# Shift and scale columns from raw fp32 blocks as stationary operand, and a tile-by-tile pipeline for the first k and v products

## The chip, the cores and the metric

The kernel runs on one NeuronCore of a Trainium2 chip. The core has a matrix engine (TensorE, PE in the profile; PEld is its loading of the stationary operand), VectorE (DVE), ScalarE (ACT), GpSimd (POOL) and SyncE (SP), which here only issues transfers; 16 DMA engines move the data. The metric is the device time of one launch in microseconds, lower is better. The runs of a kernel are summed up by their median.

## The reference, cut to what matters

One layer of a hybrid model over 1280 rows (1024 latent tokens and 256 context tokens) of 1024 features. The part that the change touches is the beginning:

```
cond_ = silu(cond)                       # two vectors: c (latent), c_ctx (context)
mod   = cond_ @ w_ada + b_ada            # 1024 x 6144; sh1, sc1, gt1, sh2, sc2, gt2
u     = rmsnorm(x, g_norm1) * (1 + sc1) + sh1
proj  = u @ w_in                         # xp, su, sv, q, k, v, o_pre, gate_pre, br_pre
```

Behind it follow a pooling branch, a spatial gating branch and a four-head mLSTM (whose gates are in gate_pre, and whose first step needs k, v and q of head 0), the merge, and a feed-forward block. All of it is fp32; the products are made from split operands, a rounded high part and a low part.

## The kernel before

**Tiling.** The rows stand in ten row tiles of 128 (`xt[0]` to `xt[9]`), in three groups: 512 rows (tiles 0 to 3), 512 (4 to 7) and 256 (8 and 9, the context). The features stand in eight feature tiles of 128 (k = 0 to 7). A feature tile of a group is made in four steps: row tiles are scaled by their norm (`scale_rows`: ACT squares and sums, DVE adds, POOL takes the power, DVE scales); PE transposes 128x128 pieces into a PSUM tile `pt_u` (`transpose_cols`); ACT writes `val_u` = `pt_u` * a + sh, with one scale and one shift for each feature; DVE splits it into `u..h` and `u..l` (`modulate_cols`). ACT also issues the transfer of `val_u` to `scr_u` in DRAM, for later stages.

**Products.** `dense` makes, for a weight matrix split into hi and lo (`load_w`), three products a feature tile: hi*h, hi*l, lo*h. In the trace they are `p_k` and `p_v`, 512 columns for groups 0 and 1 and 256 for group 2.

**Shift and scale.** Only the first 2048 columns of w_ada are needed for the first modulation: blocks 0 and 1 are the shift of feature tiles 0 to 3 and 4 to 7, blocks 2 and 3 the scale of the same tiles. SP fetches them in the order 0, 2, (weights of k0), 1, 3, each as eight tiles `wa` of 128x512 (256 KB). Each block is handled in two steps. `mod_split(b)`: ACT rounds a `wa` tile into `wah`, DVE (POOL for two tiles in eight) subtracts to `wal`, and PE multiplies with the two conditioning columns (`shl`, `sh0`) as the stationary operand: two products of 512 columns a tile into `pm`. `mod_cols(b)`: ACT copies the row result to `mrow`, four small fp32 products (`pmc`) turn it into columns, and DVE adds the bias (`sh1`) or makes (1+sc)*g (`a1`).

**Order.** From line 248 to 297 the engines are wrapped in `Pinned` (line 44 in the trace is its call): each engine takes its instructions in the order of the code. Behind line 297 a scheduler sets the order. The pinned part handles group 0 alone. Behind it come the split of the gate weights, the transfers, scaling and modulation of row tiles 4 to 9 (lines 304 to 310), the gate product `pg` (lines 322 to 331), and a chain of small steps on DVE and ACT that ends in the transposes `pc` (line 396). k0 and v0 of groups 1 and 2 are made in `head_proj(0)`, beside that chain.

Of the kernel before, what the change touches and what calls it, by code (L numbers as in the profile page):

```python
# [49 lines left out]
def hybrid_step(  # L50
# [38 lines left out]

    def load_w(src, name, raw=None, eng=V):  # L90
        raw = fetch_w(src, name) if raw is None else raw
        hi = wp.tile([P, 1024], F32R, tag="hi", name=f"hi_{name}", bufs=NHL)
        lo = wp.tile([P, 1024], F32R, tag="lo", name=f"lo_{name}", bufs=NHL)
        A.copy(hi, raw)
        eng.tensor_tensor(lo, raw, hi.bitcast(F32), ALU.subtract)
        return hi, lo
# [21 lines left out]
    def dense(ps, w, acts, g, ks=range(KT)):  # L118
        n = GROUPS[g][1]
        whi, wlo = w  # L120
        for k in ks:
            ahi, alo = acts[k][g]
            s = slice(k * P, (k + 1) * P)
            PE.matmul(ps[:, :n], whi[:, s], ahi, start=k == 0, stop=False)
            PE.matmul(ps[:, :n], whi[:, s], alo, start=False, stop=False)
            PE.matmul(ps[:, :n], wlo[:, s], ahi, start=False, stop=k == KT - 1)
# [35 lines left out]
    def norm_rows(x, n, name):  # L162
        sq = small([P, 2], f"sq_{name}")
        for hf in (0, 1):
            junk = tmp(f"junk_{name}{hf}")
            A.activation(junk, x[:, hf * 512 : hf * 512 + 512], AF.Square, accum_out=sq[:, hf : hf + 1])
# [4 lines left out]
    def transpose_cols(src, g, k, name):
        ps = ps_sd(f"pt_{name}{g}_{k}")
        for i in range(GROUPS[g][1] // P):
            PE.transpose(ps[:, i * P : (i + 1) * P], src[i][:, k * P : (k + 1) * P], ident)
        return ps

    def modulate_cols(dst, ps, g, k, a, sh, name):
        n, j = GROUPS[g][1], 1 if g == 2 else 0
        val = tmp(f"val_{name}{g}_{k}")
        A.activation(val[:, :n], ps[:, :n], AF.Identity, bias=sh[:, k, j : j + 1], scale=a[:, k, j : j + 1])  # L180
        if g < 2:
            A.dma_start(scr_u[g][k], val)
# [4 lines left out]
    def scale_rows(g):
        for i in range(GROUPS[g][0] // P, (GROUPS[g][0] + GROUPS[g][1]) // P):
            r = norm_rows(xt[i], 1, f"x{i}")
            V.tensor_scalar(xt[i], xt[i], r[:, 0:1], None, ALU.mult)  # L190

    ada = {}
    for b in (0, 2, 1, 3):
        if b == 1:
            raw_k0 = fetch_w(w_in[I_K], "k0")
        for k in range(KT):
            ada[b, k] = slot(f"wa{b}_{k}", F32)
            SP.dma_start(ada[b, k], w_ada[k * P : (k + 1) * P, b * 512 : (b + 1) * 512])
# [21 lines left out]
    def mod_split(b, ks=range(KT), behind=2):  # L220
        if b not in pms:
            pms[b] = ps_sd(f"pm{b}")
        pm = pms[b]
        for k in ks:
            wh, wl = slot(f"wah{b}_{k}"), slot(f"wal{b}_{k}")
            A.copy(wh, ada[b, k])
            (G if k in POOL_LO else V).tensor_tensor(wl, ada[b, k], wh.bitcast(F32), ALU.subtract)
            PE.matmul(pm[0:4, :], shl[:, k, :], wh, start=k == 0, stop=False)
            los.append((k, wl))
            while los and (k == KT - 1 or los[0][0] <= k - behind):  # L230
                k2, w2 = los.pop(0)
                PE.matmul(pm[0:4, :], sh0[:, k2, :], w2, start=False, stop=k2 == KT - 1)

    def mod_cols(b):
        half = b % 2
        kk = slice(half * 4, half * 4 + 4)
        mrow = mrows[half][0:4, (b // 2) * 512 : (b // 2 + 1) * 512]
        A.copy(mrow, pms[b][0:4, :])
        pmc = ps_mm(f"pmc{b}")
# [3 lines left out]
        dst = sh1 if b < 2 else a1
        V.tensor_tensor(dst[:, kk, :], pmv, bav[:, b * 4 : b * 4 + 4, :], ALU.add)
        if b >= 2:
            V.scalar_tensor_tensor(a1[:, kk, :], a1[:, kk, :], 1.0, g1v[:, kk, :], ALU.add, ALU.mult)

    V, A, G, PE = (Pinned(tc, e) for e in engines)
    scale_rows(0)
    u0 = [None] * KT  # L250

    def tr(k):
        u0[k] = transpose_cols(xt[0:4], 0, k, "u")

    def mc(k):
        modulate_cols(uT, u0[k], 0, k, a1, sh1, "u")

    mod_split(0)
    mod_split(2, (0, 1))
    mod_cols(0)  # L260
# [36 lines left out]
    V, A, G, PE = engines
    wgh = wp.tile([P, KT, 100], F32R, tag="hi", name="wg_hi", bufs=NHL)
    wgl = wp.tile([P, KT, 100], F32R, tag="lo", name="wg_lo", bufs=NHL)
    for i in range(2):  # L300
# [1 line left out]
        tc.keep_in_program_order(A.copy(wgh[:, ks], wg[i]))
        tc.keep_in_program_order(V.tensor_tensor(wgl[:, ks], wg[i], wgh[:, ks].bitcast(F32), ALU.subtract))
    for i in range(4, NT):
        SP.dma_start(xt[i], xs[i])
    for g in (1, 2):
        scale_rows(g)
        t0, n = GROUPS[g]
        for k in range(KT):
            modulate_cols(uT, transpose_cols(xt[t0 // P : (t0 + n) // P], g, k, "u"), g, k, a1, sh1, "u")  # L310
# [144 lines left out]
    hn2 = [z[:, 9010 + i * 512 : 9522 + i * 512].rearrange("p (c t) -> p c t", t=P) for i in range(2)]  # L455

    def proj(idx, name, evict, eng=V):
        w, ps = begun.pop(name, (None, None))
        w = w or load_w(w_in[idx], name, eng=eng)
        for g in range(3):  # L460
            if ps is None or g > 0:
                ps = ps_mm(f"p_{name}{g}")
                dense(ps, w, uT, g)
            evict(g, ps)

    def head_proj(h):
        tiles = {}
        kq = slot(f"kq{h}", F32)
        for nm, idx, sc in (("k", I_K, float(P) ** -0.5), ("v", I_V, 1.0), ("q", I_Q, 1.0)):
            lst = tiles[nm] = []  # L470

            def ev(g, ps):
                n = GROUPS[g][1]
                if g == 2 and nm != "v":
                    t = kq[:, 0:256] if nm == "k" else kq[:, 256:512]
                else:
                    t = slot(f"{nm}T{h}_{g}", F32)
                A.activation(t[:, :n], ps[:, :n], AF.Copy, scale=sc)
                lst.append(t)

            proj(idx + h, f"{nm}{h}", ev)
# [965 lines left out]
```

## Time and profile before

| what | value |
| --- | --- |
| median of three runs | 1984.17 us (1979.58 to 1986.23) |
| the profiled execution | 1989.21 us |
| its span | 1987.40 us |
| its mean granted PE clock | 0.989 |
| the chain that ended last | PE 40%, DVE 3%, DMA 2%, ACT 1% of the span |

The chain that ended last is work followed back from the last instruction; its share is mostly PE. The page's table of 40 slices gives the busy share in tenths: the first slice of 50 us and the last are those in which PE is not full.

```profile
PE   5999999999899999999999999999999999999997
PEclk9999999999999999999999998999999999999999
```

A line of the timeline reads: start and duration in microseconds, engine, line of the code, operation, output tile<-input tiles, shapes, count, and in brackets the idle time before it and what ended that.

### The profile page before, as it was taken

What the parts mean: (1) busy time and instruction counts of PE and PEld (TensorE: products, weight loads), DVE (VectorE), ACT (ScalarE), POOL (GpSimd) and SP (SyncE); (2) the same over time, 40 slices, a digit from 0 to 9 for tenths busy, and PEclk for the clock granted to TensorE, in tenths of its full rate; (3) what the DMA queues carried; (4) which work ended last, traced back from release to release, by engine and by line L of the source; (5) the groups of instructions that cost most, each with busy time, mean ns of one, the idle gap of its engine ahead of it and who ended that gap; (6) DMA issues with size and microseconds to landing.
All of it is one profiled execution on the core that took longest, in us unless ns stands there. A gap on an engine that the chain in (4) does not pass through costs nothing. (4 is left out here: it accounts for less than half of the span.)

```text
span 1987.4 us, 29215 instructions
## 1 busy us (share of the span) xinstructions
PE 1923.3 (97%) x10544; PEld 1656.8 (83%) x10544; DVE 1332.6 (67%) x2269; ACT 858.1 (43%) x1780; POOL 382.5 (19%) x372
## 2 busy tenths in 40 slices
PE   5999999999899999999999999999999999999997
PEld 2788888998778888878889998888888878888886
DVE  6684344448878979774566689888776654654664
ACT  6543454653143333331014565554445544443443
POOL 3000001116402324330000005445441110000002
PEclk9999999999999999999999998999999999999999
DMA  8211111112564545469634535776774586655544
GB/s 341 86 45 38 48 59 42 40 57 85 175 228 145 169 142 176 133 210 345 234 122 149 170 139 186 271 260 237 249 275 142 190 324 210 197 177 155 165 134 148
DMA packets 160642, 332.70 MB, mean 167 GB/s; under 512 B 18929, under 2 KB 41329, under 8 KB 158449
## 3 DMA queue, kind: packets, MB, share of 16 engines
q1 hardware_dynamic: 107280, 224.30, 34.6%
q10 hardware_dynamic: 38976, 52.97, 7.4%
q0 software_dynamic: 14240, 53.56, 7.3%
q8 instruction: 83, 1.36, 0.3%
q14 instruction: 63, 0.51, 0.1%
HBM read 229.53 MB, written 101.22 MB: 166 GB/s over the span
## 5 line engine op out<-in xcount | busy, mean ns | idle before, releaser
L1155 POOL TENSOR_TENSOR z<-z 128x512 f32<-128x512 f32 x64 | 98.7, 1543 | 133.7 <-DMA z<-in_w_ff 131.0
L885 DVE TENSOR_TENSOR z<-z 128x512 f32<-128x512 f32 x112 | 92.2, 824 | 2.5
L445 POOL PARTITION_ALL_REDUCE acc<-acc x16 | 55.0, 3474 | 188.5 <-DVE acc L439 117.6
L439 DVE SCALAR_TENSOR_TENSOR acc<-z,scond,acc 128x512 f32<-128x512 f32 x112 | 85.9, 815 | 0.0
L1269 POOL TENSOR_TENSOR rs_y<-rs_y,neghalf 128x1 f32<-128x1 f32 x10 | 9.4, 940 | 333.6 <-DVE rs_y L1268 333.6
L1121 ACT ACTIVATE z<-z 128x512 f32<-128x512 f32 x64 | 40.5, 632 | 76.4 <-DVE z L894 36.7
L910 ACT ACTIVATE z<-z 128x512 f32<-128x512 f32 x48 | 30.2, 632 | 71.8 <-DVE z L894 27.7
L819 ACT CAST hi_wb<-raw_wb 128x512 fp32r<-128x512 f32 x24 | 14.8, 620 | 100.7 <-PE pb L987 67.2
L131 POOL TENSOR_TENSOR rs_h<-rs_h,neghalf 128x4 f32<-128x4 f32 (+1 forms) x12 | 11.9, 992 | 207.9 <-DVE rs_h L130 207.8
L992 DVE TENSOR_TENSOR sg<-pb,sg 128x512 f32<-128x512 f32 (+1 forms) x48 | 28.9, 602 | 33.0 <-PE pb L988 31.6
L582 DVE SCALAR_TENSOR_TENSOR yc<-th,ccol,z 128x512 f32<-128x512 f32 (+1 forms) x12 | 7.9, 660 | 57.2 <-PE th L580 57.2
L1122 ACT ACTIVATE z<-z 128x512 f32<-128x512 f32 x64 | 40.3, 630 | 1.1
L670 POOL TENSOR_TENSOR z<-z 128x1024 f32<-128x1024 f32 (+13 forms) x20 | 34.8, 1750 | 14.0 <-ACT z L654 12.5
L819 ACT CAST hi_wo<-raw_wo 128x512 fp32r<-128x512 f32 x48 | 28.8, 616 | 19.9 <-PE po L1087 13.6
L1090 DVE TENSOR_TENSOR po<-po,gt 128x256 f32<-128x256 f32 x40 | 17.2, 430 | 29.3 <-PE po L1088 29.2
L1146 POOL DMA_DIRECT2D scr_s<-x x48 | 26.3, 551 | 52.0 <-DVE x L1140 47.3
L446 POOL TENSOR_TENSOR acc<-acc,bt 1x512 f32<-1x512 f32 x16 | 23.8, 1500 | 59.0 <-issue 59.0
L820 DVE TENSOR_TENSOR lo_wo<-raw_wo,hi_wo 128x512 fp32r<-128x512 f32 x48 | 32.2, 686 | 3.6 <-ACT hi_wo L819 3.6
L44 PE MATMUL pm<-wah,shl 128*4 128x512 f32 x32 | 14.7, 479 | 17.2 <-DVE s_x L44 12.5
L1093 ACT ACTIVATE po<-z 128x256 f32<-128x256 f32 x40 | 15.4, 385 | 36.9 <-DVE z L1092 35.7
L516 DVE SCALAR_TENSOR_TENSOR z<-z,dmb,kv 128x129 f32<-128x129 f32 x56 | 16.3, 344 | 21.9 <-PE kv L505 21.6
L569 DVE TENSOR_TENSOR den<-den,gcol 128x2 f32<-128x2 f32 x40 | 6.2, 159 | 35.2 <-ACT den L568 34.4
(5091 smaller groups left out, 7466.7 us busy)
## 6 DMA issues: line engine op xcount, KB each, us to landing
z<-in_w_ff SPq DMA_DIRECT2D x64, 512.0 KB, 5.5
z<-in_w_ada SPq DMA_DIRECT2D x64, 256.0 KB, 3.3
scr_t<-z POOLq DMA_DIRECT2D x16, 1024.0 KB, 4.6
z<-in_w_in SPq DMA_DIRECT2D x24, 512.0 KB, 4.4
scr_g<-z ACTq DMA_DIRECT2D x48, 256.0 KB, 2.0
sg<-scr_g SPq DMA_DIRECT2D x48, 256.0 KB, 4.6
raw_wo<-in_w_out SPq DMA_DIRECT2D x48, 256.0 KB, 3.5
scr_h<-z ACTq DMA_DIRECT2D x48, 256.0 KB, 4.0
```

The costliest lines, as they stand in the source:

```text
L439: V.scalar_tensor_tensor(acc[j], raw, scond[:, k, j : j + 1], acc[j], ALU.mult, ALU.add)
L445: G.partition_all_reduce(acc[j], acc[j], P, bass.bass_isa.ReduceOp.add)
L670: eng.tensor_tensor(at(dst, a, b), at(src, a - l, b - l), at(src, a + r_, b + r_), ALU.add)
L819: A.copy(hi, raw)
L820: V.tensor_tensor(lo, raw, hi.bitcast(F32), ALU.subtract)
L885: V.tensor_tensor(out, x, y, op)
L910: A.activation(t, t, AF.Sigmoid)
L992: V.tensor_tensor(sg[:, :n], pb[:, :n], sg[:, :n], ALU.mult)
L1121: A.activation(t, t, AF.Relu)
L1122: A.activation(t, t, AF.Square)
L1146: G.dma_start(scr_s[fp][:, i, :], t)
L1155: G.tensor_tensor(out, x, y, ALU.subtract)
```

## The change

Blocks 0 and 2 are no longer split. A new function `mod_direct` takes each raw `wa` tile as the stationary operand, 128 columns at a time, and multiplies it in fp32 with the two conditioning columns `scond` as the moving operand: the result stands in columns (`pmc`) at once. Blocks 1 and 3 go on as before. `cols_done` is the last part of the old `mod_cols`. SP fetches row tiles 4 to 7 ahead of the gate weights, and 8 and 9 behind them. POOL in place of ACT issues the transfers to `scr_u`.

The pinned order now reaches over all three groups: a loop `steps` goes through the 24 pairs of group and feature tile, in which the transposes stand four tiles and the modulation two tiles ahead of the products of k0 and v0. Row tiles are scaled one by one (`scale_row`), 8 and 9 inside the loop. k0 and v0 of all groups are finished there and written out by `evict_kqv`, taken from `head_proj`; the split of the gate weights stands behind it.

```diff
-            A.dma_start(scr_u[g][k], val)
+            nc.gpsimd.dma_start(scr_u[g][k], val)
...
-    def scale_rows(g):
-        for i in range(GROUPS[g][0] // P, (GROUPS[g][0] + GROUPS[g][1]) // P):
-            r = norm_rows(xt[i], 1, f"x{i}")
-            V.tensor_scalar(xt[i], xt[i], r[:, 0:1], None, ALU.mult)
+    def scale_row(i):
+        r = norm_rows(xt[i], 1, f"x{i}")
+        V.tensor_scalar(xt[i], xt[i], r[:, 0:1], None, ALU.mult)
...
     raw_v0 = fetch_w(w_in[I_V], "v0")
+    for i in range(4, 8):
+        SP.dma_start(xt[i], xs[i])
...
+    for i in (8, 9):
+        SP.dma_start(xt[i], xs[i])
...
+    def cols_done(b, pmv):
         half = b % 2
         kk = slice(half * 4, half * 4 + 4)
...
+        dst = sh1 if b < 2 else a1
+        V.tensor_tensor(dst[:, kk, :], pmv, bav[:, b * 4 : b * 4 + 4, :], ALU.add)
+        if b >= 2:
+            V.scalar_tensor_tensor(a1[:, kk, :], a1[:, kk, :], 1.0, g1v[:, kk, :], ALU.add, ALU.mult)
...
+    def mod_direct(b):
+        pmc = ps_mm(f"pmc{b}")
+        pmv = pmc[:, 0:8].rearrange("p (c j) -> p c j", j=2)
+        for k in range(KT):
+            for c in range(4):
+                PE.matmul(
+                    pmv[:, c, :], ada[b, k][:, c * P : (c + 1) * P], scond[:, k, :],
+                    start=k == 0 and c == 0, stop=k == KT - 1 and c == 3)
+        cols_done(b, pmv)
...
+    for i in range(4):
+        scale_row(i)
+    mod_direct(0)
     tr(0)
     tr(1)
     tr(2)
-    mod_split(2, (2, 3, 4, 5, 6, 7))
-    mod_split(1, (0, 1))
-    mod_cols(2)
-    mod_split(1, (2, 3))
+    mod_direct(2)
+    mod_split(1, (0, 1, 2, 3))
     w_k0 = load_w(None, "k0", raw_k0)
     mc(0)
+    ps_k0 = ps_mm("p_k00")
     mod_split(1, (4, 5))
     mc(1)
     tr(3)
+    dense(ps_k0, w_k0, uT, 0, (0,))
     mod_split(1, (6, 7))
-    ps_k0 = ps_mm("p_k00")
-    dense(ps_k0, w_k0, uT, 0, (0,))
     mc(2)
+    tr(4)
+    dense(ps_k0, w_k0, uT, 0, (1,))
+    mod_cols(1)
     mod_split(3, (0, 1))
-    mod_cols(1)
+    mc(3)
+    tr(5)
+    dense(ps_k0, w_k0, uT, 0, (2,))
     mod_split(3, (2, 3))
-    dense(ps_k0, w_k0, uT, 0, (1,))
-    tr(4)
-    tr(5)
     tr(6)
-    mod_split(3, (4, 5, 6, 7))
-    mc(3)
+    dense(ps_k0, w_k0, uT, 0, (3,))
+    mod_split(3, (4, 5))
     w_v0 = load_w(None, "v0", raw_v0)
+    scale_row(4)
+    mod_split(3, (6, 7))
+    scale_row(5)
+    ps_v0 = ps_mm("p_v00")
+    dense(ps_v0, w_v0, uT, 0, (0, 1, 2))
     mod_cols(3)
-    dense(ps_k0, w_k0, uT, 0, (2, 3))
+    dense(ps_v0, w_v0, uT, 0, (3,))
+    mc(4)
     tr(7)
-    ps_v0 = ps_mm("p_v00")
-    dense(ps_v0, w_v0, uT, 0, (0, 1, 2, 3))
-    for k in (4, 5, 6, 7):
-        mc(k)
-        dense(ps_k0, w_k0, uT, 0, (k,))
-        dense(ps_v0, w_v0, uT, 0, (k,))
-    begun = {"k0": (w_k0, ps_k0), "v0": (w_v0, ps_v0)}
-    V, A, G, PE = engines
+    scale_row(6)
+    mc(5)
+    scale_row(7)
...
+    steps = [(g, k) for g in range(3) for k in range(KT)]
+    begun = {"k0": (w_k0, []), "v0": (w_v0, [])}
+    kq0 = slot("kq0", F32)
+
+    def evict_kqv(nm, h, g, ps, kq):
+        n = GROUPS[g][1]
+        if g == 2 and nm != "v":
+            t = kq[:, 0:256] if nm == "k" else kq[:, 256:512]
+        else:
+            t = slot(f"{nm}T{h}_{g}", F32)
+        A.activation(t[:, :n], ps[:, :n], AF.Copy, scale=float(P) ** -0.5 if nm == "k" else 1.0)
+        return t
+
+    for at, (g, k) in enumerate(steps):
+        if (g, k) < (0, 4):
+            continue
+        if (g, k) == (1, 1):
+            scale_row(8)
+            scale_row(9)
+        if at + 4 < len(steps):
+            tr(steps[at + 4][1], steps[at + 4][0])
+        if at + 2 < len(steps):
+            mc(steps[at + 2][1], steps[at + 2][0])
+        if k == 0:
+            begun["k0"][1].append(evict_kqv("k", 0, g - 1, ps_k0, kq0))
+            begun["v0"][1].append(evict_kqv("v", 0, g - 1, ps_v0, kq0))
+            ps_k0, ps_v0 = ps_mm(f"p_k0{g}"), ps_mm(f"p_v0{g}")
+        dense(ps_k0, w_k0, uT, g, (k,))
+        dense(ps_v0, w_v0, uT, g, (k,))
+    begun["k0"][1].append(evict_kqv("k", 0, 2, ps_k0, kq0))
+    begun["v0"][1].append(evict_kqv("v", 0, 2, ps_v0, kq0))
...
```

PE, from the program's start, before (`pm` is the row product of a block, `pmc` the columns, `pt_u` a transposed tile):

```order
L44 MATMUL pm_233<-wal_5_263,sh_182 4x512
L44 MATMUL pm_233<-wal_6_269,sh_182 4x512
L44 MATMUL pm_233<-wal_7_275,sh_182 4x512
L44 MATMUL pm_282<-wah_0_283,shl 4x512
L44 MATMUL pm_282<-wah_1_288,shl 4x512
L44 MATMUL pmc_294<-cst,mrow_hi 128x2 x4
L44 MATMUL pt_u_0_300<-cst,z 128x128 x4
```

And in the changed kernel:

```order
L44 MATMUL pmc_239<-scond,wa_7_121 128x2 x4
L44 MATMUL pt_u_0_273<-cst,z 128x128 x4
L44 MATMUL pt_u_1_278<-cst,z 128x128 x4
L44 MATMUL pt_u_2_283<-cst,z 128x128 x4
L44 MATMUL pmc_288<-scond,wa_0_123 128x2 x4
L44 MATMUL pmc_288<-scond,wa_1_125 128x2 x4
```

The 16 products of 512 columns of each of blocks 0 and 2, and four turns, are gone; eight rows of four two-column products stand in their place for each block, and PE reads `wa` as it landed. The first row of block 1 (`pm_323`) now stands behind both blocks.

DVE, from the end of the first scaling to the first split tile, in the changed kernel (`sh_82` and `a_81` are shift and scale, `wal` the low parts of block 1):

```order
L44 TENSOR_TENSOR sh_82<-pmc_239,ccol 128x8
L44 TENSOR_TENSOR a_81<-pmc_288,ccol 128x8
L44 SCALAR_TENSOR_TENSOR a_81<-a_81,ccol 128x8
L44 TENSOR_TENSOR wal_0_325<-wa_0_141,wah_0_324 128x512
L44 TENSOR_TENSOR wal_1_330<-wa_1_143,wah_1_329 128x512
L44 TENSOR_TENSOR wal_3_341<-wa_3_147,wah_3_340 128x512
L95 TENSOR_TENSOR lo_k_347<-raw_k_139,hi_k_346 128x1024
L44 CAST u0h_353<-val_u_0_350 128x512
```

Before, twelve subtractions for blocks 0 and 2 and the first two of block 1 stood ahead of `a_81`; now none does, so every subtraction of block 1 comes after it.

PE, at the products of feature tile 4 of group 0, in the changed kernel (in `pt_u1_0` the first number is the group, the second the feature tile):

```order
L44 MATMUL p_v00_519<-u3h0_435,lo_v0_480 128x512
L44 MATMUL pt_u0_7_547<-cst_76,z_74 128x128 x4
L44 MATMUL pt_u1_0_582<-cst_76,z_74 128x128 x4
L44 MATMUL p_k00_357<-u4h0_543,hi_k0_346 128x512
L44 MATMUL p_k00_357<-u4l0_544,hi_k0_346 128x512
L44 MATMUL p_k00_357<-u4h0_543,lo_k0_347 128x512
L44 MATMUL p_v00_519<-u4h0_543,hi_v0_479 128x512
```

Before, no transpose of the second group stood ahead of the products of tile 4: they came after tile 7. The row `pt_u1_0` reads row tiles 4 to 7 after their scaling.

More of the change, by code (lines that the diff above doesn't have):

```diff
@@ L232, in mod_split, with mod_cols @@
                 PE.matmul(pm[0:4, :], sh0[:, k2, :], w2, start=False, stop=k2 == KT - 1)
-    def mod_cols(b):
+    def cols_done(b, pmv):
         half = b % 2
         kk = slice(half * 4, half * 4 + 4)
-        mrow = mrows[half][0:4, (b // 2) * 512 : (b // 2 + 1) * 512]
+        dst = sh1 if b < 2 else a1
+        V.tensor_tensor(dst[:, kk, :], pmv, bav[:, b * 4 : b * 4 + 4, :], ALU.add)
+        if b >= 2:
+            V.scalar_tensor_tensor(a1[:, kk, :], a1[:, kk, :], 1.0, g1v[:, kk, :], ALU.add, ALU.mult)
+    def mod_cols(b):
+        mrow = mrows[b // 2][0:4, 0:512]
         A.copy(mrow, pms[b][0:4, :])
@@ L242, in mod_cols, with tr, mc @@
             PE.matmul(pmv[:, c, :], mrow[:, c * P : (c + 1) * P], cst[0:4, 3 * P : 3 * P + 2], start=True, stop=True)
[L243 to L246, printed above, removed]
-    V, A, G, PE = (Pinned(tc, e) for e in engines)
[L249 to L260, printed above, removed]
+        cols_done(b, pmv)
[7 more added lines that the diff above has]
+                    start=k == 0 and c == 0, stop=k == KT - 1 and c == 3)
+        cols_done(b, pmv)
+    V, A, G, PE = (Pinned(tc, e) for e in engines)
+    u0 = {}
+    def tr(k, g=0):
+        t0, n = GROUPS[g]
+        u0[g, k] = transpose_cols(xt[t0 // P : (t0 + n) // P], g, k, "u")
+    def mc(k, g=0):
+        modulate_cols(uT, u0[g, k], g, k, a1, sh1, "u")
+    for i in range(4):
+        scale_row(i)
+    mod_direct(0)
     tr(0)
@@ L301, in hybrid_step @@
         ks = slice(4 * i, 4 * i + 4)
[L302 to L310, printed above, removed]
+        A.copy(wgh[:, ks], wg[i])
+        V.tensor_tensor(wgl[:, ks], wg[i], wgh[:, ks].bitcast(F32), ALU.subtract)
+    V, A, G, PE = engines
     bgt = cp.tile([36, 2], F32, name="bgt")
@@ L457, in proj @@
     def proj(idx, name, evict, eng=V):
-        w, ps = begun.pop(name, (None, None))
-        w = w or load_w(w_in[idx], name, eng=eng)
+        w = load_w(w_in[idx], name, eng=eng)
         for g in range(3):
-            if ps is None or g > 0:
-                ps = ps_mm(f"p_{name}{g}")
-                dense(ps, w, uT, g)
+            ps = ps_mm(f"p_{name}{g}")
+            dense(ps, w, uT, g)
             evict(g, ps)
@@ L467, in head_proj @@
         tiles = {}
-        kq = slot(f"kq{h}", F32)
-        for nm, idx, sc in (("k", I_K, float(P) ** -0.5), ("v", I_V, 1.0), ("q", I_Q, 1.0)):
-            lst = tiles[nm] = []
[L472 to L481, printed above, removed]
+        kq = kq0 if h == 0 else slot(f"kq{h}", F32)
+        for nm, idx in (("k", I_K), ("v", I_V), ("q", I_Q)):
+            if f"{nm}{h}" in begun:
+                tiles[nm] = begun[f"{nm}{h}"][1]
+                continue
+            lst = tiles[nm] = []
+            proj(idx + h, f"{nm}{h}", lambda g, ps: lst.append(evict_kqv(nm, h, g, ps, kq)))
         return tiles["k"], tiles["v"], tiles["q"]
```

## The prediction

> **What bounds the kernel now.** I read the page's totals first, then the PE's waits over the whole run, then windows of the start. The page's first lines:
>
> ```profile
> span 1987.4 us, 29215 instructions
> PE 1923.3 (97%) x10544; PEld 1656.8 (83%) x10544; DVE 1332.6 (67%) x2269; ACT 858.1 (43%) x1780; POOL 382.5 (19%) x372
> ```
>
> PE is busy for 97% of the span and idle for 64 us. PE's waits (who waits, for whom: us, times, longest) and two windows of a hundred microseconds say where:
>
> ```profile
> PE pm L44 <- DVE s_x L44: 12.5, 1, 12.5
> PE pm L44 <- ACT wah L44: 4.7, 1, 4.7
> PE pc L396 <- DVE z L384: 2.8, 1, 2.8
> ```
>
> The windows give length, then PE, PEld, DVE, ACT, POOL busy (x instructions), granted clock, DMA share and GB/s:
>
> ```profile
> 200.00:300.00 100.00, 100.00 (x594) 88.21 (x593) 44.02 (x126) 51.85 (x137) 3.72 (x4) 1.00 0.16 50
> 500.00:600.00 100.00, 90.27 (x457) 73.96 (x456) 74.60 (x113) 31.30 (x53) 17.33 (x19) 0.97 0.57 198
> ```
>
> The largest waits lie in the opening and at the gate chain (pc). Later PE has little slack, so I let a microsecond won or lost before the gates pass to the end. The opening by stage:
>
> ```profile
> 0.00:30.50 30.50, 15.25 (x66) 6.36 (x66) 18.07 (x40) 19.65 (x42) 11.49 (x16) 1.00 0.96 359
> 30.50:50.48 19.98, 14.58 (x67) 8.34 (x67) 14.64 (x23) 11.56 (x21) 4.02 (x3) 0.83 0.79 306
> 50.48:60.08 9.60, 9.60 (x45) 7.86 (x45) 7.36 (x18) 8.33 (x21) 1.31 (x3) 1.00 0.39 150
> 60.08:93.06 32.98, 28.85 (x146) 21.23 (x145) 19.44 (x48) 14.82 (x30) 2.85 (x4) 0.95 0.17 64
> 93.06:133.20 40.14, 37.36 (x205) 32.42 (x204) 34.61 (x25) 20.05 (x23) 2.47 (x5) 1.00 0.17 53
> ```
>
> The cuts are four events: T0, the first modulation (30.50); the modulation of tile 4 (50.48), which needs blocks 1 and 3; the end of tile 7 of the first group (60.08); the end of the gate product (93.06). I work out the change at each.
>
> **Stage 1, T0.** Single rows of the timeline (lines between them left out here and below): start, duration, engine, line, what, and in brackets idle time and its releaser.
>
> ```profile
> 11.16 1.64 SPq L198 DMA_DIRECT2D wa<-in_w_ada  x3
> 11.84 5.75 ACT L44 CAST wah<-wa 128x512 fp32r<-128x512 f32 x10
> 28.61 1.05 PE L44 MATMUL pmc<-cst,mrow_hi 4*128 4x2 f32 x8 [0.20 <-ACT mrow_hi L44]
> 30.50 0.78 ACT L44 ACTIVATE val_u<-pt_u,sh,a 128x512 f32<-128x512 f32 x1
> 37.08 1.05 PE L44 MATMUL pt_u<-cst,z 128*128 128x128 f32 x4
> 18.31 0.63 PE L44 MATMUL pm<-wal,sh 128*4 128x512 f32 x1
> 18.74 0.63 PE L44 MATMUL pm<-wah,shl 128*4 128x512 f32 x1
> ```
>
> Block 0's first tile has landed by 11.84, when ACT casts it; ACT squared rows until then. I take 11.2: SP has at most so many transfers in flight, and goes on there. What goes for two blocks: 32 casts, 32 subtractions, 32 thin products and 8 turns. What comes: 64 fp32 products of two columns. An fp32 product is two passes, for the row at 28.61 has 8 records for 4 products; a pass is a load of 128 columns and a matmul of 2. There it takes (1.05-0.25)/7 = 0.115 us. A block is 32 products, 64 passes: 7.4 us.
>
> But that row ran at full clock. At 18.31 the matmuls of 512 follow each other at 0.43 us, against 0.23 at 57.36 (rows of stage 3): PE starts at half clock, though the window's column reads 1.00, as it does wherever the record holds no change yet. Would these passes raise it? The trace has a stretch like them, 20 transposes of 36 columns (windows again, then rows):
>
> ```profile
> 133.05:136.46 3.41, 3.24 (x24) 3.20 (x25) 3.37 (x10) 0.21 (x1) 0.00 (x0) 0.50 0.04 9
> 136.46:139.88 3.42, 3.42 (x15) 3.13 (x14) 3.29 (x13) 2.71 (x3) 0.00 (x0) 0.50 0.04 10
> ```
>
> ```profile
> 133.22 2.32 PE L396 MATMUL pc<-cst,z 36*128 36x36 f32 x20 [2.80 <-DVE z L384]
> 142.15 0.81 PE L396 MATMUL pc<-cst,z 36*128 36x36 f32 x10
> ```
>
> In the first window PE is occupied for 95% of 3.41 us, yet the clock stays at 0.50 through the next; after that one, of full matmuls, it rises. So short columns behind weight loads did not count. The direct blocks move 2 columns a load, less still: I take half clock for both. A pass of pc costs (2.32-0.30)/19 = 0.106 there against (0.81-0.23)/9 = 0.065 at full clock, 1.6 times; between that and 2 I take 1.8: 64 x 0.115 x 1.8 = 13.3 us a block. Bounds: 7.4 (the clock does nothing) and 14.7 (twice).
>
> The three transposed tiles stand between the blocks: 12 transposes at 0.21 (the row at 37.08, half clock) make 2.5. The last pmc to T0 took 30.50-29.66 = 0.84. So T0 = 11.2+13.3+2.5+13.3+0.8 = 41.1, **10.6 later** (bounds 28.4, with transposes at full clock 1.5, and 43.9: -2.1 and +13.4). ACT and DVE are freed of 64 instructions, but nothing of theirs was T0's limit that is not replaced.
>
> The Trainium skill (TensorE: Matmul & The Clock Gate, Part 1: The HAM clock gate) says that PE starts at half rate and that some 3.4 us of sustained activity releases it. Taken as occupied time, that would free the clock early in block 0; the windows above disagree. Its section on LDWEIGHTS gives columns over 1.2 GHz, an estimate of 107 ns for 128: 64 of them would be 6.8 us a block, and T0 about 28 us.
>
> **Stage 2, T0 to tile 4.**
>
> ```profile
> L44 DVE TENSOR_TENSOR wal<-wa,wah x24: 676/680/1787, 14.0 to 46.0; 128x512 fp32r<-128x512 f32 x24
> ```
>
> ```profile
> 30.99 1.21 DVE L95 TENSOR_TENSOR lo_k<-raw_k,hi_k 128x1024 fp32r<-128x1024 f32 x1
> 39.36 0.42 DVE L44 CAST u2h<-val_u 128x512 fp32r<-128x512 f32 x1
> 39.89 0.69 DVE L44 TENSOR_TENSOR u2l<-val_u,u2h 128x512 fp32r<-128x512 f32 x1
> 57.12 0.75 DVE L190 TENSOR_SCALAR z<-z,rs_x 128x1024 f32<-128x1024 f32 x1 [0.65 <-POOL rs_x L131]
> 34.74 1.14 ACT L44 CAST wah<-wa 128x512 fp32r<-128x512 f32 x2 [3.47 <-DMA wg<-in_w_gate]
> 50.48 0.78 ACT L44 ACTIVATE val_u<-pt_u,sh,a 128x512 f32<-128x512 f32 x1 [1.54 <-DVE a L44]
> ```
>
> DVE's row for the scale now stands ahead of all of block 1's subtractions, so none is done before T0. From T0 DVE does, in this order: 12 subtractions of 0.68 (8.2), lo_k and lo_v (2.4), four tiles of 1.1 (4.4), two scaled row tiles at 1.05 (2.1), shift and scale (0.5): 17.6 us. Waits in the order: 1.4 for pmc1, two powers on POOL at 0.6, and 1.7 because nine products of v0 (2.1) and pmc3 (1.05) stand between the last subtraction and the scale. Sum 21.9 against 19.98: **+1.9**. The 3.5 us that ACT lost at 34.74 is won: its DMA of scr_u, queued ahead of the casts, had to let an earlier transfer land; on POOL it delays POOL's next rows instead. Without that move this stage would be up to 3.5 longer. At zero, DVE waits hidden, it is -0.9; two more waits at their size make +4.
>
> **Stage 3, tile 4 to tile 7.**
>
> ```profile
> 44.53 1.47 PE L44 MATMUL pt_u<-cst,z 128*128 128x128 f32 x12
> 54.76 0.62 ACT L166 ACTIVATE junk_x<-z 128x512 f32<-128x512 f32 x1
> 55.99 0.62 ACT L166 ACTIVATE junk_x<-z 128x512 f32<-128x512 f32 x1
> 56.55 0.54 POOL L131 TENSOR_TENSOR rs_x<-rs_x,neghalf 128x1 f32<-128x1 f32 x1 [11.62 <-DVE rs_x L130]
> 57.36 0.39 PE L44 MATMUL p_k<-u6h,hi_k 128*128 128x512 f32 x1
> 57.59 0.39 PE L44 MATMUL p_k<-u6l,hi_k 128*128 128x512 f32 x1
> ```
>
> A new wait comes here. PE's transposes of the second group's tile 0 stand ahead of the products of tile 4, and need row tiles 4 to 7 scaled. Tiles 6 and 7 are squared on ACT (1.23 each: 54.76 to 55.99) behind val4 and val5 (0.7 each): 3.9 us after val4 starts. Sums on DVE until about 5.2, since tile 5's split is ahead; POOL's power for tile 7 is queued behind the DMA of val6, then 0.54; scaling 0.75: about 6.7. Queued behind PE's wait are all products of tiles 4 to 7, although tile 4 is split at 2. Four steps follow, each six products at 0.23 and four transposes at 1.47/12: 1.87, together 7.5. And PE idles some 6 us, more than the 3.41 of a window, so the clock drops; it costs half of a window, 1.7. Sum 15.9 against 9.60: **+6.3** (without the clock +4.6; with two windows +8).
>
> **Stage 4, tile 7 to the end of the gates.**
>
> ```profile
> 92.94 0.27 PE L329 MATMUL pg<-u7c,wg_lo 128*100 128x256 f32 x1
> 93.05 0.28 PE L124 MATMUL p_k<-u0c,hi_k 128*128 128x256 f32 x1
> 93.17 0.28 PE L125 MATMUL p_k<-u0c,hi_k 128*128 128x256 f32 x1
> ```
>
> Before, 33.0 us, with 24 short products of k, 24 long and 24 short of v and six of q left for later: 28 long at 0.23 and 50 short at (93.17-92.94)/2 = 0.115 are 12.2, so 45.2 for equal work. After: eight steps of 1.87 and eight of 0.94 (six short products, two transposes), 22.5; gates 48 x 0.23 + 24 x 0.115 = 13.8; q 1.2; for evictions, row tiles 8 and 9 and the gate weights' split, now late on ACT, 3. Sum 40.5: **-4.7** (bounds -7.7 with no stall, -1.7 with twice).
>
> **Stage 5, the gate chain.** Its DVE work is the same, less one split of weights (1.2), and PE has q, o0 and k1, 38 us, beside it against 37.4 in the window from 93.06. **-1.0.**
>
> **Sum.** 10.6+1.9+6.3-4.7-1.0 = +13.1. The profiled execution took 1989.21 us around its span of 1987.40; it would be 2002.3. The median of the runs shown is 1984.17, 5 lower, so **1997**.
>
> **The rivals.** A measurement tells 0.3%, some 6 us, from no change.
>
> *The loads count as activity*, so PE warms inside block 0 (some 17 us), T0 is near 31, stage 3 loses its 1.7: +0.5+1.9+4.6-4.7-1.0 = +1.3, 1985. For it: PE is never idle there. Against: the window at 133.05. 0.12. This is what the Trainium skill's rule cited above would give.
>
> *Faster: the loads run at full clock and at the transposes' rate*, 0.065 a pass. A block would be 4.2, less than its transfer. The 16 tiles of 262 KB land at 0.65 us each:
>
> ```profile
> 11.50:15.00 3.50, 1.63 (x3) 0.25 (x3) 2.65 (x5) 3.50 (x8) 2.11 (x3) 1.00 1.05 406
> ```
>
> the last at 11.2+15 x 0.65 = 21, T0 about 22.4: -8.1+1.9+4.6-4.7-1.0 = -7.3, 1977. It decides once T0 is before some 24. Against: pmc's 0.115. 0.12.
>
> *The change is absorbed*: PE's idle 9.7 us in 500 to 600 shrinks by what the start loses, if a chain there doesn't begin on PE: 13.1-9.7, some 1988. Against: its inputs are PE's. 0.08.
>
> **How the numbers follow.** The forecast has 0.68; with its terms' bounds (T0 at a factor of 1.6 to 2, the stalls) it covers 1990 to 2005. Rivals one and three, within 0.3%, 0.20; the second 0.12. The range 1984 to 2006 leaves out the second and a tail. Faster 0.12, within 0.20, slower 0.68.
>
> **What would show it.** The passes of pmc in the direct blocks: 0.2 us each at a clock of 0.5, block 0 ending near 24.5, val_u first at 41. Then PE waiting some 6 us on DVE's z ahead of the second group's tile 0. A first val_u before 31, or a clock of 1.0 in the blocks, makes the forecast wrong; so does a stage 4 above 43 us, the other way.

## The result, and the profile after

The changed kernel takes 1998.45 us in the median of five runs (1992.50 to 2001.68), the kernel of before 1984.17 (1979.58 to 1986.23). The ratio is 1.0080 with a 95% interval of 1.0060 to 1.0101, that is 12 to 20 us slower. (It is estimated from all the runs; the quotient of the two medians is 1.0072, 14 us.) The profiled execution took 2001.68 us.

The first two lines of the page of the changed kernel, and three of PE's waits over the whole run (who waits, for whom: us, times, longest):

```profile
span 1999.9 us, 29347 instructions
PE 1936.7 (97%) x10624; PEld 1678.4 (84%) x10624; DVE 1315.9 (66%) x2257; ACT 847.6 (42%) x1761; POOL 387.2 (19%) x384
```

```profile
PE pmc L44 <- DVE s_x L44: 11.1, 1, 11.1
PE pt_u L44 <- DVE z L44: 5.4, 2, 2.9
PE pm L44 <- DVE wal L44: 3.1, 4, 2.1
```

PE is busy 13.4 us longer than before, and ACT and DVE are busy 10.5 and 16.7 us less: the work went to the engine that sets the end. The first wait is the start of the program; PE's 5.4 us for row tiles (z) in the pinned part are new.

Five windows, cut at the same events as before (first modulation, modulation of tile 4, end of tile 7 of the first group, then one cut at 109.60; columns as before):

```profile
0.00:41.51 41.51, 30.42 (x142) 29.99 (x143) 5.62 (x26) 10.14 (x24) 5.46 (x12) 1.00 0.96 369
41.51:65.75 24.24, 19.01 (x86) 10.33 (x85) 19.09 (x31) 13.58 (x28) 8.34 (x9) 1.00 0.26 88
65.75:82.11 16.36, 10.93 (x46) 8.59 (x45) 9.53 (x20) 8.04 (x16) 5.68 (x9) 0.79 0.28 113
82.11:109.60 27.49, 25.80 (x150) 21.36 (x149) 17.31 (x39) 15.49 (x31) 4.20 (x7) 1.00 0.16 59
109.60:146.00 36.40, 36.40 (x191) 30.41 (x190) 20.72 (x13) 14.06 (x16) 0.92 (x1) 1.00 0.15 51
```

The first three stages are longer than before by 11.0, 4.3 and 6.8 us. In the first, PE is occupied from 11 us on, nearly all of it with weight loads (PEld 29.99). In the third it stands still for a third of the time, and the clock drops.

Stage 1, rows of PE's and ACT's timeline (start, duration, engine, line, what):

```profile
11.09 13.79 PE L44 MATMUL pmc<-scond,wa 128*128 128x2 f32 x64 [11.09 <-DVE s_x L44]
24.74 2.80 PE L44 MATMUL pt_u<-cst,z 128*128 128x128 f32 x12
27.33 13.65 PE L44 MATMUL pmc<-scond,wa 128*128 128x2 f32 x64
41.51 0.78 ACT L44 ACTIVATE val_u<-pt_u,sh,a 128x512 f32<-128x512 f32 x1 [15.45 <-DVE a L44]
```

Each block has 64 passes in 13.65 to 13.79 us, one per 0.213 us (13.79 less the last pass's 0.35, by 63). For block 2 and the transposes ahead of it ACT waits 15.5 us and DVE 15.9. The clock column reads 1.00 in this window only because the record holds no change yet: the first products of 512 columns behind block 2 start 0.43 us apart (42.08, 42.51, 42.94), and 0.23 apart from 44.06 on. So PE was at half clock through both blocks, and came to full clock only under the wide products.

Stage 3, PE's timeline at the new wait:

```profile
65.99 0.82 PE L44 MATMUL pt_u<-cst,z 128*128 128x128 f32 x6
69.69 0.33 PE L44 MATMUL pt_u<-cst,z 128*128 128x128 f32 x1 [2.88 <-DVE z L44]
72.56 0.47 PE L44 MATMUL pt_u<-cst,z 128*128 128x128 f32 x1 [2.55 <-DVE z L44]
72.69 0.78 PE L44 MATMUL p_k<-u4h,hi_k 128*128 128x512 f32 x1
73.27 0.63 PE L44 MATMUL p_k<-u4l,hi_k 128*128 128x512 f32 x1
73.69 0.63 PE L44 MATMUL p_k<-u4h,lo_k 128*128 128x512 f32 x1
```

The transposes of the second group's tile 0 stop twice, once for row tile 6 and once for 7, with tile 4's products behind them. Afterwards matmuls of 512 columns follow at 0.42 us (73.27 to 73.69), not 0.23: half clock, until about 78.

### The profile page after: what moved, and what is told of

It reads as the page before. It is cut to its first block, busy times and chain, and to the rows that moved or that the text cites. A ratio compares the mean times of both kernels' runs of the same rounds, so it can differ in the third digit from the quotient of the medians.

```text
span 1999.9 us, 29347 instructions
## 1 busy us (share of the span) xinstructions
PE 1936.7 (97%) x10624; PEld 1678.4 (84%) x10624; DVE 1315.9 (66%) x2257; ACT 847.6 (42%) x1761; POOL 387.2 (19%) x384
## 5 line engine op out<-in xcount | busy, mean ns | idle before, releaser
L921 DVE TENSOR_TENSOR z<-z 128x512 f32<-128x512 f32 x112 | 96.9, 866 | 2.5
L1157 ACT ACTIVATE z<-z 128x512 f32<-128x512 f32 x64 | 40.5, 633 | 69.8 <-DVE z L930 34.8
L706 POOL TENSOR_TENSOR z<-z 128x256 f32<-128x256 f32 (+13 forms) x20 | 37.2, 1872 | 26.9 <-ACT z L690 14.2
L44 PE MATMUL pmc<-scond,wa 128*128 128x2 f32 x128 | 27.4, 351 | 11.1 <-DVE s_x L44 11.1
L44 PEld LDWEIGHTS pmc<-scond,wa 128*128 128x128 f32 x128 | 27.5, 333 | 11.1 <-DVE s_x L44 11.1
```

Of the source, the lines that this page charges most:

```text
L44: return self.tc.keep_in_program_order(getattr(self.eng, op)(*args, **kw))
L921: V.tensor_tensor(out, x, y, op)
```

## The experiments

Theory A: the 128 weight loads of the direct blocks at 0.213 us a pass set the first modulation; the wait for row tiles 6 and 7 adds to it; what the start loses reaches the end. The rivals are named with each run. All runs stand in one table, with the times of four events in the profiled execution (us from the start): the first modulation (val_u), that of tile 4, the end of the products of tile 7 of the first group, and "sv", the first product of a stage some 300 us later. Ahead of sv every kernel has done the same work, but for the form of blocks 0 and 2 and the added matmuls of runs 4 and 8.

| kernel | median us | ratio to before, 95% interval | first val_u | tile 4 | tile 7 ends | first sv |
| --- | --- | --- | --- | --- | --- | --- |
| before | 1984.17 | 1 | 30.5 | 50.5 | 60.1 | 358.0 |
| changed | 1998.45 | 1.0080 (1.0060 to 1.0101) | 41.5 | 65.8 | 82.1 | 373.7 |
| 1 blocks 0 and 2 split again | 1989.93 | 1.0031 (1.0018 to 1.0045) | 31.0 | 53.9 | 69.8 | 363.3 |
| 2 direct blocks alone | 1987.30 | 1.0024 (1.0014 to 1.0033) | 42.3 | 58.3 | 67.9 | 365.2 |
| 3 changed, norms of tiles 6, 7 early | 1991.37 | 1.0042 (1.0027 to 1.0057) | 41.4 | 65.6 | 74.7 | 366.6 |
| 4 changed, matmuls ahead of block 0 (late) | 2007.50 | 1.0124 (1.0109 to 1.0140) | 47.9 | 72.2 | 88.3 | 379.8 |
| 5 before, scr_u issued by POOL | 1975.50 | 0.9968 (0.9958 to 0.9979) | 31.9 | 48.6 | 58.3 | 354.3 |
| 6 = 1 and 3 | 1979.54 | 0.9993 (0.9982 to 1.0005) | 31.3 | 54.3 | 63.4 | 354.9 |
| 7 changed, no subtraction on POOL | 1997.44 | 1.0086 (1.0069 to 1.0103) | 42.0 | 67.0 | 83.0 | 374.9 |
| 8 changed, matmuls ahead of block 0 (early) | 1996.34 | 1.0067 (1.0050 to 1.0084) | 40.4 | 64.6 | 80.9 | 372.6 |
| 9 = 6, block 3 finished first | 1978.41 | 0.9984 (0.9974 to 0.9995) | 30.4 | 50.2 | 60.4 | 353.7 |
| 10 = 2 and 5 | 1982.63 | 0.9996 (0.9983 to 1.0010) | 41.1 | 57.1 | 66.8 | 360.9 |

On the chips of runs 1 to 10 the kernel of before had medians of 1982.14 to 1982.39, so differences below are taken between ratios where chips differ. One thing in the sv column differs from execution to execution: beside the gate chain, between tile 7 and sv, the granted clock is half for 3.4 us in the changed kernel and in runs 4, 5, 8 and 10, for 6.8 us in the kernel of before and in runs 2, 3, 6 and 7, and for 10.2 us in runs 1 and 9. Run 9 shows what such a stretch is worth, so differences of 1 or 2 us at sv prove nothing by themselves.

**1. Only the direct blocks undone** (and the row buffer that `mod_cols` then needs, not shown).

```diff
-    mod_direct(0)
+    mod_split(0)
+    mod_split(2, (0, 1))
+    mod_cols(0)
     tr(0)
...
-    mod_direct(2)
-    mod_split(1, (0, 1, 2, 3))
+    mod_split(2, (2, 3, 4, 5, 6, 7))
+    mod_split(1, (0, 1))
+    mod_cols(2)
+    mod_split(1, (2, 3))
```

> The changed kernel with blocks 0 and 2 split and multiplied as 512-column row products again; the new pipeline, the queue of scr_u and the order of row tiles stay. Theory A (the direct blocks' 128 weight loads at 0.213 us set the first modulation, and what the start loses reaches the end one to one): the first val_u falls from 41.5 back to some 30.5, the wait for row tiles 6 and 7 (5.4 us of PE) stays, and the time is 1984 to 1989 us against 1998. Rival B (the loss sits in the new pipeline, and the direct blocks are absorbed by what follows): 1994 us or more, although val_u is early.

The first modulation is 10.5 us earlier than in the changed kernel, tile 7 12.3, sv 10.4, and the ratio falls by 0.49%, some 10 us; the wait for row tiles stays (5.4 us). The median is 1 us above theory A's range, and 4 below the rival's: most of the loss sits in the direct blocks. What is left, 0.31%, belongs to the new order.

**2. Only the direct blocks, in the old order.**

```diff
-    mod_split(0)
-    mod_split(2, (0, 1))
-    mod_cols(0)
+    cols_done(0, mod_direct(0))
     tr(0)
...
-    mod_split(2, (2, 3, 4, 5, 6, 7))
+    pmv2 = mod_direct(2)
     mod_split(1, (0, 1))
-    mod_cols(2)
+    cols_done(2, pmv2)
```

> The kernel of before with blocks 0 and 2 made directly from the raw tiles, and nothing else changed. Theory A: the first val_u at some 41.5 instead of 30.5; of these 11 us up to 3.5 come back, because the transfer that ACT waited for at 34.7 will have landed long before; 1990 to 1996 us. Rival B: within 4 us of 1984.

The first modulation is 11.8 us later, and as expected part of it comes back before tile 4, which is 7.8 later: ACT's wait for a transfer, which the prediction quotes at 34.7, is gone (0.4 us of idle is left at each transfer). The time rose by 0.24%, 5 us: less than theory A expected. Its median is in rival B's range (it is 5 us above the kernel of before on the same chip), although the opening lost what theory A says. Sv is 7.3 us later; where 2 us of that come back behind sv stays open. Run 10 returns to this.

**3. The norms of row tiles 6 and 7 ahead of block 3's columns.**

```diff
     scale_row(5)
+    r6, r7 = norm_rows(xt[6], 1, "x6"), norm_rows(xt[7], 1, "x7")
...
+    V.tensor_scalar(xt[6], xt[6], r6[:, 0:1], None, ALU.mult)
+    V.tensor_scalar(xt[7], xt[7], r7[:, 0:1], None, ALU.mult)
     mc(4)
     tr(7)
-    scale_row(6)
     mc(5)
-    scale_row(7)
```

> The changed kernel with the norms of row tiles 6 and 7 taken ahead of the last shift-and-scale block, and their scaling on DVE directly behind that block's scale, ahead of the split of tile 4. Theory A: PE's 5.4 us of waiting on DVE's z and the half clock behind it (about 1.7 us) go, tile 7 of the first group ends some 6 us earlier, 1991 to 1993 us. Rival D (the wait only moves: to the products of tile 4, whose split now stands behind two scalings, or to block 3): 1996 us or more.

PE's timeline at the same place:

```profile
65.83 1.39 PE L44 MATMUL pt_u<-cst,z 128*128 128x128 f32 x8
67.22 0.50 PE L44 MATMUL p_k<-u4h,hi_k 128*128 128x512 f32 x1
67.95 0.50 PE L44 MATMUL p_k<-u4l,hi_k 128*128 128x512 f32 x1 [0.23 <-DVE u4l L44]
```

The eight transposes run through, tile 4's products start 5.5 us earlier, and at full clock. Tile 7 ends 7.4 us earlier, sv is 7.1 earlier, the ratio falls by 0.38% (7.5 us). The wait and its half clock are worth all of that; rival D falls.

**4. Matmuls to raise the clock, late.**

```diff
+    wu = slot("wu")
+    V.memset(wu.bitcast(F32), 1.0)
...
+    pwu = ps_sd("pwu")
+    for i in range(20):
+        PE.matmul(pwu, wu[:, 0:P], wu, start=True, stop=True)
     for i in range(4):
         scale_row(i)
     mod_direct(0)
```

> The changed kernel with 20 matmuls of 512 columns on a tile of ones while PE has nothing to do, from about 1 to 10 us; their result is not used. Theory A (the passes cost 0.213 because PE is at half clock): the first block's passes start at about 0.115. If the clock then stays, the first val_u is at 28 to 29 and the time 1985 to 1987 us; if it falls again within the first block, since loads with two columns do not count as activity, the gain is a part of one block, 2 to 6 us. Rival C (0.213 is the price of a load of 128 raw fp32 columns at any clock): no change, 1998 us.

The fill of ones landed on DVE behind the scaling of the first rows, so the matmuls ran at 15.1, not at 1, and everything came 6 us later; the time tests nothing. The rows do. PE's timeline, and windows (length, PE, PEld, DVE, ACT, POOL, clock):

```profile
15.07 6.67 PE L44 MATMUL pwu<-wu 128*128 128x512 f32 x20 [15.07 <-DVE wu L209]
21.57 9.72 PE L44 MATMUL pmc<-scond,wa 128*128 128x2 f32 x64
31.15 2.80 PE L44 MATMUL pt_u<-cst,z 128*128 128x128 f32 x12
33.74 13.65 PE L44 MATMUL pmc<-scond,wa 128*128 128x2 f32 x64
```

```profile
21.50:23.50 2.00, 2.00 (x21) 1.96 (x19) 0.00 (x0) 0.97 (x2) 0.00 (x0) 1.00 1.06 407
23.50:25.50 2.00, 2.00 (x20) 2.00 (x20) 0.00 (x0) 1.88 (x4) 0.95 (x1) 1.00 1.06 407
25.50:27.50 2.00, 2.00 (x13) 2.00 (x13) 0.00 (x0) 0.57 (x1) 0.31 (x1) 0.60 1.06 407
27.50:29.50 2.00, 2.00 (x11) 2.00 (x11) 0.00 (x0) 0.00 (x0) 0.00 (x0) 0.50 1.05 404
```

Block 0 begins at 20 passes in 2 us, 0.1 us each, at full clock. Within some 4 us the granted clock falls to 0.5 although PE is occupied all the time, and then 2 us hold 11 passes. Block 2 runs at half throughout, and its passes take the 0.213 us of the changed kernel. So the price of a pass does go with the clock (rival C falls), and passes with two columns do not keep the clock up.

**5. Only the issue of scr_u moved, on the kernel of before.**

```diff
-            A.dma_start(scr_u[g][k], val)
+            nc.gpsimd.dma_start(scr_u[g][k], val)
```

> The kernel of before with the transfers to scr_u issued by POOL in place of ACT, nothing else changed. Theory A (ACT's 3.5 us of standing still behind such a transfer at 34.7 holds up block 1's casts and with them tile 4): tile 4's modulation moves from 50.5 to 47 to 49, and the time is 1.5 to 3.5 us below before. Rival E (DVE sets that stretch): within 1 us of before.

ACT's rows from the first modulation on, with no idle time between them (casts left out):

```profile
31.94 0.78 ACT L44 ACTIVATE val_u<-pt_u,sh,a 128x512 f32<-128x512 f32 x1
33.65 0.78 ACT L44 ACTIVATE val_u<-pt_u,sh,a 128x512 f32<-128x512 f32 x1
35.35 0.78 ACT L44 ACTIVATE val_u<-pt_u,sh,a 128x512 f32<-128x512 f32 x1
```

From the first modulation to tile 4 it takes 16.7 us, against 20.0 before: the 3.3 us are won in the stage where ACT stood still. The first modulation itself is 1.4 later here, so tile 4 and tile 7 are 1.9 and 1.8 earlier, and sv 3.7. Of the difference between these two, 1.4 us arise from the end of the gate product to sv, where the clock is half for 3.4 us here and for 6.8 before. The ratio 0.9968 is faster than before beyond its interval, by 6 us, more than theory A's 3.5; rival E falls. This is the lowest median of the study. What it gains beyond the opening stays open.

**6. Runs 1 and 3 together.**

> Blocks 0 and 2 split again and the norms of row tiles 6 and 7 early: the new pipeline without the two losses. Theory A: the first val_u at 31, no wait of PE for row tiles 6 and 7, some 7 us less than the kernel that has the blocks split alone: within 3 us of before (1980 to 1985 us). Rival D (with an early first val_u, the wait moves to DVE or to the split of block 3): 1987 us or more.

1979.54 us, 0.38% below run 1, as run 3 was below the changed kernel; sv is 8.4 us earlier than in run 1. The two losses add up, and theory A's 1980 to 1985 is met but for half a microsecond. The new order with neither is level with before, yet 0.25% slower than run 5, which shares the issue of scr_u and the split blocks. At sv the two are 0.6 us apart, so the opening does not explain that.

**7. All subtractions on DVE.**

```diff
-POOL_LO = (2, 5)
+POOL_LO = ()
```

> The changed kernel with all subtractions of blocks 1 and 3 on DVE (four more of 0.68 us), none on POOL. Theory F (the rows of DVE that take 1.5 us in place of 0.43 or 0.69 between the first val_u and tile 4 stand still until POOL's subtraction ends): CAST u0h, CAST u3h and the subtraction u3l take their usual 0.43, 0.43 and 0.69; 3.2 us are won and 2.7 spent, so the time stays within 2 us of the changed kernel's 1998. Rival G (those rows are slow for a reason of their own, as transfers that land in SBUF): they stay at 1.5, and 2 to 4 us are lost.

First the changed kernel, DVE and POOL:

```profile
44.25 1.51 DVE L44 CAST u0h<-val_u 128x512 fp32r<-128x512 f32 x1
53.25 1.52 DVE L44 CAST u3h<-val_u 128x512 fp32r<-128x512 f32 x1
54.81 1.65 DVE L44 TENSOR_TENSOR u3l<-val_u,u3h 128x512 fp32r<-128x512 f32 x1
43.40 2.08 POOL L44 TENSOR_TENSOR wal<-wa,wah 128x512 fp32r<-128x512 f32 x1 [0.18 <-ACT wah L44]
52.98 2.92 POOL L44 TENSOR_TENSOR wal<-wa,wah 128x512 fp32r<-128x512 f32 x2
```

And run 7, DVE:

```profile
45.33 0.42 DVE L44 CAST u0h<-val_u 128x512 fp32r<-128x512 f32 x1
53.85 0.42 DVE L44 CAST u3h<-val_u 128x512 fp32r<-128x512 f32 x1
54.30 0.69 DVE L44 TENSOR_TENSOR u3l<-val_u,u3h 128x512 fp32r<-128x512 f32 x1
```

The long rows are gone with POOL's subtractions: DVE's three instructions had stood still until one of POOL's ended (45.5, 54.5 and 55.9; POOL's last row holds two), and ended 0.3 to 0.6 us behind it. Theory F holds, rival G falls. The time doesn't move (1.0086 against 1.0080): 3.15 us were won and four subtractions added, and the scale of block 3 waited 3.3 us for PE in place of 1.8, so stage 2 has 25.0 us in place of 24.2. That last part is the clock: in this execution it was half from 61.4 to 64.8, and six of the nine products of v0 ahead of block 3's columns took 0.43 us each (they start at 61.95, 62.37, 62.80 and so on), where the changed kernel has 0.23. The Trainium skill (SBUF — State Buffer, section SBUF: two separate sides) says that VectorE and GpSimd share a port pair that one instruction holds to its end; these rows agree with it.

**8. Matmuls to raise the clock, early.**

```diff
+    pwu = ps_sd("pwu")
+    for i in range(10):
+        PE.matmul(pwu[:, 0:384], ident, cst[:, 0:384], start=True, stop=True)
     for i in range(4):
         scale_row(i)
```

> The changed kernel with ten fp32 matmuls of 384 columns on the constants ahead of block 0, while PE has nothing to do; their result is not used. Theory A with what the late warm-up showed (about 40 passes at 0.107, then 0.213 again, the granted clock falling to 0.5 with PE occupied): if these warm PE, block 0 takes some 9.5 us, block 2 still 13.6, the first val_u some 4 us earlier, 1993 to 1996 us. If they don't count as activity either, nothing changes (1998 us) or the block starts later.

```profile
3.71 9.06 PE L44 MATMUL pwu<-cst 128*128 128x384 f32 x20 [3.71 <-DMA cst<-in_consts]
12.61 11.18 PE L44 MATMUL pmc<-scond,wa 128*128 128x2 f32 x64
26.25 13.65 PE L44 MATMUL pmc<-scond,wa 128*128 128x2 f32 x64
```

The added matmuls lasted to 12.6, 1.5 us beyond the landing of the first tile. Block 0 took 11.2 us and not 13.8, block 2 still 13.65; the first modulation and sv are 1.1 and 1.2 us earlier, less than expected. In the time that can't be told from nothing (the intervals of 1.0067 and 1.0080 overlap). The added matmuls are fp32 as the passes are, but 384 columns wide, and behind them block 0 began with 20 passes in 2 us: the fp32 form alone is not what holds the clock down.

**9. Block 3 first.** Run 6, with block 3's subtractions ahead of v0's weights and of all row scaling, its columns ahead of v0's products, and the transposes of the second group's tile 0 behind tile 4's products.

```diff
-    mod_split(3, (4, 5))
+    mod_split(3, (4, 5, 6, 7))
     w_v0 = load_w(None, "v0", raw_v0)
...
+    mod_cols(3)
...
-    dense(ps_v0, w_v0, uT, 0, (0, 1, 2))
-    mod_cols(3)
-    dense(ps_v0, w_v0, uT, 0, (3,))
+    dense(ps_v0, w_v0, uT, 0, (0, 1, 2, 3))
...
+        if (g, k) == (0, 4):
+            tr(0, 1)
```

> The kernel with blocks 0 and 2 split, in the new pipeline, with block 3 finished first: its last subtractions ahead of v0's weights and of the scaling of row tiles 4 to 7, its columns ahead of v0's products, and the transposes of the second group's tile 0 behind the products of tile 4. Theory A (in the new order DVE's 3 us of row scaling and PE's nine products of v0 stand in the chain to the last scale): tile 4's modulation moves from 54.3 to some 50.5, tile 7 of the first group ends 2 to 3 us earlier than in the kernel with the rows early (63.3), and the time is 1975 to 1978 us. Rival H (the scheduled part behind gives the gain back, by waits that come with another order): 1979 us or more.

In the opening theory A holds: tile 4 at 50.2, tile 7 ends at 60.4, 2.9 us earlier than in run 6, and the gate product ends 2.9 earlier too. Of these 2.9 us sv keeps 1.2, and the median 1.1, between the two ranges; its interval and run 6's overlap. The windows from the end of the gate product to sv, of run 6 and of this run, each with its stretch at half clock, show where the rest went:

```profile
101.70:354.88 253.18, 249.49 (x1483) 220.46 (x1481) 133.12 (x307) 119.41 (x285) 15.95 (x15) 0.99 0.14 44
141.40:148.30 6.90, 6.72 (x42) 6.46 (x42) 6.81 (x22) 1.97 (x3) 0.00 (x0) 0.51 0.18 64
```

```profile
98.79:353.65 254.86, 251.16 (x1482) 222.01 (x1481) 133.29 (x307) 119.44 (x285) 15.94 (x15) 0.98 0.14 43
139.50:149.80 10.30, 10.30 (x56) 9.67 (x55) 7.55 (x23) 3.75 (x7) 0.00 (x0) 0.50 0.07 14
```

PE has the same number of products in both and waits as long, but is busy 1.7 us longer in run 9, with 3.4 us more at half clock. So the loss is the clock in these two executions, and not, as rival H has it, waits that come with another order. Two of PE's waits of this run, and one of run 5 for the same products, show something else, namely what the new order costs against the old:

```profile
PE p_xp L124 <- DVE mt L800: 3.5, 1, 3.5
PE sv L653 <- ACT z L569: 1.5, 1, 1.5
```

```profile
PE p_xp L124 <- DVE mt L757: 2.5, 2, 1.5
```

Run 6 and the changed kernel have these waits of 3.5 and 1.5 us as well, and none of the kernels in the old order waits for z at sv. Whether they come from the order that the scheduler now chooses was not tried.

**10. Direct blocks on run 5.** Run 2's diff and run 5's together.

> The kernel of before with POOL issuing the transfers to scr_u, and blocks 0 and 2 made directly. Theory A (the direct blocks cost what the first val_u is later, some 11 us; alone they seemed to cost 5, since the same delay covered ACT's wait for a transfer): 1985 to 1989 us, the same as with ACT issuing them. Rival I (the direct blocks cost only 5 us, and POOL's issuing is worth 6 in any case): 1979 to 1983 us.

Against run 5 the first modulation is 9.2 us later, tile 7 8.5, sv 6.6, and the median 7.1 (the ratio 0.28%, 5.5 us). It lies in rival I's range by the time, yet not by its reason: tile 7 does come 8.5 us later, with nothing covering it. Some 2 us of that are made up between tile 7 and the end of the gate product: for the same 147 products PE is busy 29.3 us in run 5, at half clock from 70.5 to 73.9, and 28.2 in run 10, at full clock; the rest is shorter waits. So in the old order the direct blocks cost 5 to 7 us, in the new one 10 (run 1).

## Why the prediction was right, step by step

The forecast was 1997, and the measured median is 1998.45; the direction and the mechanisms are the ones that the runs show: run 1 takes back the loss of the direct blocks, run 3 that of the wait. Three terms were mis-sized: stage 2 by +2.4 us, stage 4 by -2.2 and stage 5 by +1.6.

*Stage 1* was +10.6, and is +11.0. The start (11.09) and the half clock came as worked out. The factor 1.8 was low: a pass takes 0.213, about twice the 0.1 that run 4 shows at full clock (20 passes in 2 us), so each block was 0.4 us longer than the 13.3 worked out. That short columns behind loads don't raise the clock was read from the transposes of the gate chain, and run 4 shows it for the passes themselves. The prediction's other price, 107 ns a load, is what a pass takes at full clock in run 4, and not at the clock that these passes had. The rival that loads count as activity falls for these passes: PE was occupied in every window of run 4 while the clock fell. With it falls here the reading of the Trainium skill's rule that the prediction cites (TensorE: Matmul & The Clock Gate, Part 1: The HAM clock gate), with sustained activity taken as occupied time. The Trainium skill (TensorE: Matmul & The Clock Gate, Part 4: PE-mode transpose) says of transposes that they don't count as busy in the same way; this fits the rows of the gate chain, and the direct passes, which are no transposes, behave alike.

*Stage 2* was +1.9, and is +4.3. The step that was too small is the list of DVE's work: it left out that DVE stands still while POOL subtracts. DVE is busy for 19.09 us, 3.15 of which are the three long rows (1.51, 1.52 and 1.65, less 0.42, 0.42 and 0.69), and idle for 5.15 where 4.3 were allowed; its own work is 15.9 and not 17.6. Together 24.2. The bounds of this step were too narrow: +4.3 lies just beyond its +4, and its lower bound of -0.9 does not follow from the terms, since the listed work without any wait is 17.6, 2.4 below the 19.98 of before. The move of scr_u to POOL, which the step counted as 3.5 us won, is worth 3.3 in this stage of the old order (run 5).

*Stage 3* was +6.3, and is +6.8. PE idled for 5.4 us at the transposes of the second group's tile 0, where some 6 were worked out, and lost a little more to the clock: from the start of tile 4's products to the end of tile 7 it took 9.4 us, against 7.5 in run 3, so 1.9 where 1.7 were allowed. Run 3 shows that both go with the late norms.

*Stage 4* was -4.7. The gates end at 120.4, 38.3 us after tile 7, so it is -6.9: of the 3 us set aside for evictions, row tiles and the split of the gate weights, PE idled 1.7 (27.49 less 25.80 in the fourth window), and none in the fifth; the products took 36.6 where 37.5 were added up.

*Stage 5* was -1.0. From the gates' end to sv the kernel of before has 252.7 us (from 105.3, where its k0 and v0 would end) and the changed one 253.3: +0.6. The gain that was argued from one split less does not show. What the step left out are PE's waits: 2.8 us before, and 4.8 in the changed kernel, 1.5 of them for ACT's z right ahead of sv, a wait that all kernels of the new order have and none of the old. Against that stand 3.4 us less at half clock beside the gate chain.

The sum at sv is 11.0+4.3+6.8-6.9+0.6 = 15.8, against 13.1 forecast, and the ratio says 16. That the median came within 1.5 us of the forecast is in part luck. The sum is 2.7 too small, and would be further off if stages 2 and 4 had not missed in opposite directions; and behind sv, where the prediction has no term, the profiled execution of the changed kernel took 1626.2 us and that of before 1629.5.

That a microsecond lost in the opening reaches the end held here within the error, and in run 3 (7.4 us at tile 7, 7.1 at sv, 7.5 by the ratio). It held less well elsewhere: run 1 won 12.3 us at tile 7 and 10 in the end, run 10 lost 8.5 and then 5.5 to 7, and run 5 won 1.8 and then 6. The rival of absorption was wrong for this change as a whole. For the direct blocks in the old order it has a little for it, 7.3 us at sv and 5 in the ratio (run 2), but most of what came back there came back before sv.

## What to carry to other kernels

Weight loads with two moving columns behind them did not keep PE's clock up here, so whoever replaces wide products by such passes should price them at half rate. When one edit holds several, take each alone: here one line (another queue for a transfer) gained 0.3%, and was buried under two that lost 0.5% and 0.4%. In a hand-written order, look behind each instruction that waits for a far engine: transposes that stood four tiles ahead stopped products that were ready.

## What the runs showed of the hardware

The granted clock fell to 0.50 with PE occupied in each window (run 4), within some 4 us from the first of the two-column passes. A pass with 128 raw columns to load takes 0.213 us at half clock (changed kernel) and half of it at full (runs 4 and 8). Two casts and a subtraction of DVE stood still until a subtraction on POOL ended (1.5 us in place of 0.42, 1.65 in place of 0.69), and did not once POOL had none (run 7). Beside the gate chain the clock was half for 3.4, 6.8 or 10.2 us, depending on the run, and 3.4 us more of it cost 1.7 us of PE's time (runs 6 and 9).
